# Two 256-column matmuls for each 512-column matmul of the down products in a hybrid decoder trunk

## The chip, the cores and the metric

The kernel runs on one core of one Trainium2 chip. The metric is the device time of one execution in microseconds (us), measured by the host's runs; the profile is one further execution recorded by the hardware profiler. Engines are named as in the profile: PE is the matrix engine (PEld its loading of stationary weights, which overlaps the matmuls), DVE the vector engine, ACT the scalar engine, POOL and SP the other two, SP issuing nearly all DMAs. A change of 0.2% is 3.7 us here.

## The reference

A decoder trunk of two layers over 512 tokens of width 1024. Each layer adds half a SwiGLU channel mixer, then a token mixer (latent attention in layer 0, sparse attention in layer 1), then half a second channel mixer; a norm ends it. The change touches the four channel mixers alone:

```python
def swiglu(x, w_gate, w_up, w_down):
    return (jax.nn.silu(x @ w_gate) * (x @ w_up)) @ w_down

for i in range(DEPTH):                      # DEPTH = 2
    h = h + 0.5 * swiglu(rmsnorm(h, ffn_norm_a[i]), ffn_a_w_gate[i], ffn_a_w_up[i], ffn_a_w_down[i])
    ...                                     # token mixer
    h = h + 0.5 * swiglu(rmsnorm(h, ffn_norm_b[i]), ffn_b_w_gate[i], ffn_b_w_up[i], ffn_b_w_down[i])
return rmsnorm(h, final_norm)
```

The hidden width is 2816, 22 blocks of 128. `@ w_down` is what the text calls the down product.

## The kernel before

Activations lie transposed: channels on the 128 partitions, the 512 tokens along the free axis, so the residual is eight tiles `h` of 128x512. A matmul of full precision is made as three in a rounded format: each operand is split into a high part (ACT copies it, `split`, L205) and a low part (DVE subtracts, L206), and `mm3` (L195) issues high weights by high data (L197), high by low (L198) and low by high (L199) into one PSUM bank.

A channel mixer is `ffn` (L424). For hidden blocks 0 to 2 gate and up are plain products: `plain1` (L396, matmuls L401 to L403) makes each 512-column bank in two halves of 256 columns, left and right tokens apart. For blocks 3 to 21 `wsums` (L341) and `product` (L381, matmuls L386 to L388) make the two from seven products over quarter blocks, all 256 columns wide, into the banks `px`, `pq` and `pg`. ACT copies the partial sums out (L543 to L550); a later product goes on in the same bank, so PE's product 6 into `px` waits for ACT's L543. `gate` and `act` (L430, L440) then make the activated block, split as `ah[f]` and `al[f]`, tiles of 128x512.

The down product of three finished hidden blocks and one of the eight output chunks is a `unit` (L459): SP loads a slab `wdr`, ACT and DVE split it into the two tiles `wd` (three buffers each), `down` (L451) issues three times `mm3`, nine matmuls of 512 columns, into a bank `pd`, and `add` (L456) adds that bank to the residual on DVE. Eight units belong to three hidden blocks; two or three of them follow each block's seven products on PE (L556). One such stretch of units is called a down run below. The last four hidden blocks of a mixer are multiplied at its end, chunk by chunk, with slabs from `wslab` (tile `w`). The fourth mixer ends in `last` (L582) instead: there the activations are the stationary operand and the weight slabs the moving one; the last bank of its last token block is made in two parts of 256 columns, 24 matmuls on L612 to L614.

The prediction speaks of where tiles lie in a partition. `wtiles` shifts slabs by `PAD` = 16 elements, 64 bytes, by kind:

```python
o, d = {"x": (0, 0), "act": (3 * PAD, 0), "half": (PAD, 2 * PAD)}[kind]
return t[:, o : o + 1024], t[:, o + d + 1024 : o + d + 2048]
```

"half" slabs feed the 256-column products, "act" slabs the 512-column products with `ah` and `al`. By the built program's allocation the byte address of every `ah`, `al`, `wd` and "act" tile leaves 192 on division by 256, high and low parts alike. The `x` and `four` tiles, the moving data of the 256-column products, leave 0, and their weight tiles leave 64 or 192. The text calls the address of the weights that are loaded next, less that of the data that moves meanwhile, modulo 256, the **offset**: it is 0 in the 512-column down products and 64 or 192 in every 256-column product of the mixers. In `last`, five of six loads have offset 0 and the sixth 128.

The order on each engine is set when the program is built, by a scheduler that goes by estimated durations; `issue_after` fixes some points. Each engine runs its own list in order.

Of the kernel before, what the change touches and what calls it, by code (L numbers as in the profile page):

```python
# [19 lines left out]
S = 512  # L20
# [26 lines left out]
HS = S // 2  # L47
# [14 lines left out]
class Kern:  # L62
# [361 lines left out]
    def ffn(self, idx, gain_next, ap, tp):  # L424
        nc, a = self.nc, self.a
        self.scr, self.fp = (tp, "sq", 1), tp
        ah, al, ht, row = {}, {}, [], None
# [22 lines left out]

        def down(p, w, b0, b1):  # L451
            for k in range(b0, b1):
                last = self.mm3(p, w[0][:, k - b0], w[1][:, k - b0], ah[k], al[k], k == b0, k == b1 - 1)
            return last

        def add(c, p):  # L456
# [2 lines left out]
        def unit(tag, b0, c):  # L459

            w = [ap.tile([P, NG * P], F32R, tag=t, bufs=3, name="wd").rearrange("p (k c) -> p k c", c=P) for t in ("dh", "dl")]
            raw = ap.tile([P, NG * P], F32, tag="dr", bufs=2, name="wdr")
            nc.sync.dma_start(raw, a["w_down"][idx, c, :, b0 * P : (b0 + NG) * P])
            with self.tc.issue_after(self.spread.ins) if idx % 2 and not b0 else nullcontext():
                self.split(raw.rearrange("p (k c) -> p k c", c=P), *w)
            p = self.bank(tag, "pd")
            down(p, w, b0, b0 + NG)
            add(c, p)
# [61 lines left out]
        for f in range(PLAIN, NF):  # L530
# [6 lines left out]
            w = self.wsums(idx, f)  # L537
            x, q, g = self.bank("S", "px")[:, :HS], self.bank("mm", "pq")[:, :HS], self.bank("T", "pg")
# [20 lines left out]
        if gain_next == "fin":  # L559

            hs, out = [self.parts(self.four(F32)) for _ in range(4)], []
            for t in range(4):
                for b in range(2):
                    p = self.mm_bank("ph")
# [9 lines left out]
        for c in self.order:  # L574
            p = self.mm_bank("pd")
            down(p, self.wslab(a["w_down"][idx, c, :, tail * P :], (NF - tail, P), "act"), tail, NF)
            add(c, p)
            self.norm_chunk(c)
            if ahead and c == self.order[-1]:
                self.ahead.append(ahead())  # L580
# [942 lines left out]
```

## Time and profile before

| what | value |
|---|---|
| median of three runs | 1866.52 us (1866.4 to 1866.85) |
| the profiled execution, its own time | 1865.65 us |
| span in the profile, first to last instruction | 1863.9 us |
| granted PE clock, mean | 0.999 |
| PE busy | 1849.9 us, 99% of the span, 12448 matmuls |
| PEld busy | 1686.5 us, 90% |
| DVE busy | 1506.2 us, 81% |
| ACT busy | 1068.5 us, 57% |

The four channel mixers run from about 0 to 356, 546 to 884, 884 to 1222 and 1520 to 1863 us. A matmul's duration in the profile is longer than the time until the next one starts, since matmuls overlap in the array; what a matmul costs a stream is the spacing of starts, read from the timeline. In the grouped view each row gives line, engine, operation, output<-inputs, shape and count, then busy us and mean ns of one, then the idle time ahead of the group.

### The profile page before, as it was taken

The numbers are of one execution on the slowest core, as the hardware profiler recorded it, in microseconds if no ns is written. First come the engines' busy times: TensorE is split into PE (matmuls) and PEld (weight loads), VectorE is DVE, ScalarE is ACT, GpSimd is POOL, SyncE is SP. The second block draws the span as 40 slices with busy tenths as digits, with TensorE's granted clock in tenths as the row PEclk, the third lists the DMA queues.
The fourth block names the chain that finished last, engine by engine and source line by source line (L and its number), as shares of the span: only waits on it lengthen the run. The fifth ranks groups of instructions, "written<-read, shape, count | busy, mean of one in ns | idle before, by whom it ended". The sixth has DMA issues, their size and how long they took to land.

```text
span 1863.9 us, 32992 instructions
## 1 busy us (share of the span) xinstructions
PE 1849.9 (99%) x12448; PEld 1686.5 (90%) x12448; DVE 1506.2 (81%) x2810; ACT 1068.5 (57%) x1997; POOL 297.4 (16%) x370
## 2 busy tenths in 40 slices
PE   9999999999999999999999999999999999999998
PEld 9999999878889999998999999988888889999997
DVE  8988886688779888886898887676878888888885
ACT  7555553577666555554655555445776865555554
POOL 0000000258830000001000000022666620000000
PEclk9999999999999999999999999999999999999999
DMA  6333331334433333322433332162433133333321
GB/s 238 125 114 102 102 91 47 117 103 105 115 124 112 116 102 104 112 74 64 142 120 110 107 107 80 44 180 84 108 109 103 41 118 122 114 104 105 104 78 69
DMA packets 84335, 196.38 MB, mean 105 GB/s; under 512 B 10944, under 2 KB 38464, under 8 KB 84176
## 3 DMA queue, kind: packets, MB, share of 16 engines
q1 hardware_dynamic: 81664, 191.34, 33.7%
q10 hardware_dynamic: 2512, 2.93, 0.5%
q8 instruction: 98, 1.61, 0.4%
q14 instruction: 61, 0.50, 0.1%
HBM read 178.44 MB, written 2.16 MB: 97 GB/s over the span
## 4 chain that ended last, share of the span: by engine, by line
PE 92%; DVE 3%; ACT 1%; issue 1%; POOL 1%; DMA 1%; SPq 0%; ACTq 0%; DVEq 0%; POOLq 0%
PE pd L198 8%; PE pd L197 8%; PE pd L199 8%; PE px L386 6%; PE px L388 5%; PE px L387 5%; PE pg L386 4%; PE pg L387 4%; PE pg L388 4%; PE pq L386 4%; PE pq L387 4%; PE pq L388 4%; PE o L1326 2%; PE pt L1299 2%; PE po L197 1%; PE po L199 1%
## 5 line engine op out<-in xcount | busy, mean ns | idle before, releaser
L198 PE MATMUL pd<-al,wd 128*128 128x512 f32 x576 | 225.1, 391 | 0.0
L197 PE MATMUL pd<-ah,wd 128*128 128x512 f32 x576 | 224.9, 390 | 0.0
L199 PE MATMUL pd<-ah,wd 128*128 128x512 f32 x576 | 224.6, 390 | 0.0
L289 POOL TENSOR_TENSOR s<-s,sq 128x512 f32<-128x512 f32 x38 | 54.9, 1445 | 1051.2 <-ACT sq L285 1051.2
L206 DVE TENSOR_TENSOR w<-wr,w 128x1024 fp32r<-128x1024 f32 x72 | 88.1, 1224 | 132.9 <-ACT w L205 132.6
L386 PE MATMUL px<-four,wh 128*128 128x256 f32 x608 | 168.4, 277 | 0.4 <-ACT pg L543 0.3
L388 PE MATMUL px<-four,wl 128*128 128x256 f32 x608 | 168.1, 277 | 0.2 <-DVE wl L206 0.2
L386 PE MATMUL pq<-four,wh 128*128 128x256 f32 x608 | 167.9, 276 | 0.0
L387 PE MATMUL px<-four,wh 128*128 128x256 f32 x608 | 167.9, 276 | 0.0
L388 PE MATMUL pq<-four,wl 128*128 128x256 f32 x608 | 167.8, 276 | 0.0
L387 PE MATMUL pq<-four,wh 128*128 128x256 f32 x608 | 167.8, 276 | 0.0
L457 DVE SCALAR_TENSOR_TENSOR h<-pd,h 128x512 f32<-128x512 f32 x216 | 147.5, 683 | 13.7 <-PE pd L199 13.6
L205 ACT ACTIVATE wd<-wdr 128x384 fp32r<-128x384 f32 x192 | 99.2, 519 | 98.5 <-ACT wd L205 58.2
L199 PEld LDWEIGHTS pd<-ah,wd 128*128 128x128 f32 x576 | 108.2, 188 | 22.7
L176 ACT ACTIVATE w<-wr 128x1024 fp32r<-128x1024 f32 (+3 forms) x89 | 80.8, 908 | 82.9 <-PE pd L199 19.2
L197 PEld LDWEIGHTS pd<-ah,wd 128*128 128x128 f32 x576 | 108.1, 188 | 20.5
L198 PEld LDWEIGHTS pd<-al,wd 128*128 128x128 f32 x576 | 108.1, 188 | 19.5
L178 DVE TENSOR_TENSOR w<-wr,w 128x1024 fp32r<-128x1024 f32 (+3 forms) x75 | 78.4, 1046 | 48.9 <-ACT w L176 48.7
L717 ACT ACTIVATE p<-p,small 128x512 f32<-128x512 f32 (+2 forms) x192 | 106.9, 558 | 19.1 <-DVE small L716 15.4
L386 PEld LDWEIGHTS px<-four,wh 128*128 128x128 f32 x608 | 114.1, 188 | 1.7 <-ACT pg L543 0.8
L388 PEld LDWEIGHTS px<-four,wl 128*128 128x128 f32 x608 | 114.1, 188 | 0.8 <-DVE wl L206 0.6
L386 PEld LDWEIGHTS pq<-four,wh 128*128 128x128 f32 x608 | 114.1, 188 | 0.4 <-ACT uq L545 0.4
(379 smaller groups left out, 6153.9 us busy)
## 6 DMA issues: line engine op xcount, KB each, us to landing
wr<-in_w_gu SPq DMA_DIRECT2D x93, 512.0 KB, 3.3
ru<-in_w_gu SPq DMA_DIRECT2D x76, 512.0 KB, 4.1
wdr<-in_w_down SPq DMA_DIRECT2D x192, 192.0 KB, 2.4
wr<-in_w_down SPq DMA_DIRECT2D x24, 256.0 KB, 2.6
wr<-in_mla_w_o SPq DMA_DIRECT2D x8, 512.0 KB, 3.6
th<-btab_d SPq DMA_DIRECT2D x16, 256.0 KB, 3.8
wr<-in_nsa_w_q SPq DMA_DIRECT2D x8, 512.0 KB, 3.9
wr<-in_nsa_w_o SPq DMA_DIRECT2D x8, 512.0 KB, 3.8
```

The costliest lines, as they stand in the source:

```text
L176: self.copied = nc.scalar.activation(wh[:, m], raw[:, m], AF.Copy)
L178: nc.vector.tensor_tensor(wl[:, m], raw[:, m], f32v(wh[:, m]), op=ALU.subtract)
L197: mm(out, wh, xh, start=first, stop=False)
L198: mm(out, wh, xl, start=False, stop=False)
L199: return mm(out, wl, xh, start=False, stop=last)
L205: nc.scalar.activation(hi, src, AF.Copy)
L206: (nc.gpsimd if pool else nc.vector).tensor_tensor(lo, src, f32v(hi), op=ALU.subtract)
L386: mm(out, wh[:, p], xh, start=first and p == 0, stop=False, skip_group_check=True)
L387: mm(out, wh[:, p], xl, start=False, stop=False, skip_group_check=True)
L388: mm(out, wl[:, p], xh, start=False, stop=last and p == KP - 1, skip_group_check=True)
L457: nc.vector.scalar_tensor_tensor(self.h[c], p, 0.5, self.h[c], op0=ALU.mult, op1=ALU.add)
L717: nc.scalar.activation(p_sb[:, :n], p_sb[:, :n], AF.Exp, bias=nm, scale=-1.0, accum_out=sm)
```

## The change

Inside `down`, each 512-column `mm3` becomes two triples of 256 columns, first for the left half of the bank and then for the right half. The weights and the order of the hidden blocks stay; nothing else in the kernel is edited. `down` serves the units and the mixers' ends, not `last`.

```diff
         def down(p, w, b0, b1):
             for k in range(b0, b1):
-                last = self.mm3(p, w[0][:, k - b0], w[1][:, k - b0], ah[k], al[k], k == b0, k == b1 - 1)
+                wh, wl = w[0][:, k - b0], w[1][:, k - b0]
+                for x in range(0, S, HS):
+                    o, xh, xl = p[:, x : x + HS], ah[k][:, x : x + HS], al[k][:, x : x + HS]
+                    nc.tensor.matmul(o, wh, xh, start=k == b0 and x == 0, stop=False, skip_group_check=True)
+                    nc.tensor.matmul(o, wh, xl, start=False, stop=False, skip_group_check=True)
+                    last = nc.tensor.matmul(o, wl, xh, start=False, stop=k == b1 - 1, skip_group_check=True)
             return last
```

Lines after it are five higher in the changed kernel (L543 is L548 there). The first place is PE at the start of a down run of the first mixer, behind the last product into `pg`; `pd` is the down bank, `wd` with the lower number the high weights. Before:

```order
L387 MATMUL pg_2006<-x_153,wh_1996 128x256
L388 MATMUL pg_2006<-x_153,wl_1997 128x256
L197 MATMUL pd_2109<-ah_1277,wd_2103 128x512
L198 MATMUL pd_2109<-al_1278,wd_2103 128x512
L199 MATMUL pd_2109<-ah_1277,wd_2104 128x512
L197 MATMUL pd_2109<-ah_1456,wd_2103 128x512
L198 MATMUL pd_2109<-al_1457,wd_2103 128x512
```

And PE at the same place now:

```order
L387 MATMUL pg_2204<-x_153,wh_2194 128x256
L388 MATMUL pg_2204<-x_153,wl_2195 128x256
L456 MATMUL pd_2307<-ah_1376,wd_2301 128x256
L457 MATMUL pd_2307<-al_1377,wd_2301 128x256
L458 MATMUL pd_2307<-ah_1376,wd_2302 128x256
L456 MATMUL pd_2307<-ah_1376,wd_2301 128x256
L457 MATMUL pd_2307<-al_1377,wd_2301 128x256
L458 MATMUL pd_2307<-ah_1376,wd_2302 128x256
L456 MATMUL pd_2307<-ah_1582,wd_2301 128x256
L457 MATMUL pd_2307<-al_1583,wd_2301 128x256
```

The three matmuls of a hidden block stand twice, and the loads of weights, one ahead of each matmul, are six instead of three. Otherwise PE's order is the same in the whole program, but for a few matmuls that change places in the first two blocks of the first mixer.

The scheduler also moves some instructions on the other engines, in the channel mixers alone. The second place is ACT in the second mixer, around 610 to 616 us of the profile before: `wd<-wdr` are splits of down slabs that wait for SP's loads, `pg<-px` is the copy for which PE's product 6 waits. Before:

```order
L205 ACTIVATE wd<-wdr 128x384
L205 ACTIVATE wh<-s_7358 128x512
L205 ACTIVATE wd<-wdr 128x384
L205 ACTIVATE ah<-tu 128x512
L205 ACTIVATE wd<-wdr 128x384
L543 ACTIVATE pg<-px 128x256
L205 ACTIVATE wh<-ru 128x1024
L545 ACTIVATE uq<-pq 128x256
```

And ACT there now:

```order
L205 ACTIVATE wd<-wdr 128x384
L205 ACTIVATE wh<-s_7958 128x512
L205 ACTIVATE wh<-ru 128x1024
L205 ACTIVATE wd<-wdr 128x384
L205 ACTIVATE ah<-tu 128x512
L548 ACTIVATE pg<-px 128x256
L205 ACTIVATE wd<-wdr 128x384
L550 ACTIVATE uq<-pq 128x256
```

The copy `pg<-px` now stands ahead of the third slab's split instead of behind it, and the split `wh<-ru` has moved ahead of two slab splits. On DVE the matching subtractions move by one or two places in most blocks; on SP a `wdr` load changes places with a load of gate or up weights in a few blocks at the start of each mixer; POOL keeps its order.

## The prediction

> **What bounds the kernel now.** I read the page first, for the engine that sets the time: its busy times.
>
> ```profile
> span 1863.9 us, 32992 instructions
> PE 1849.9 (99%) x12448; PEld 1686.5 (90%) x12448; DVE 1506.2 (81%) x2810; ACT 1068.5 (57%) x1997; POOL 297.4 (16%) x370
> ```
>
> PE is busy 99% of the span, so what counts is how fast matmuls follow each other. The groups by form give what the change touches.
>
> ```profile
> L198 PE MATMUL pd<-al,wd 128*128 128x512 f32 x576 | 225.1, 391 | 0.0
> L197 PE MATMUL pd<-ah,wd 128*128 128x512 f32 x576 | 224.9, 390 | 0.0
> L199 PE MATMUL pd<-ah,wd 128*128 128x512 f32 x576 | 224.6, 390 | 0.0
> ...
> L199 PE MATMUL pd<-ah,w 128*128 128x512 f32 x96 | 37.3, 389 | 0.0
> L197 PE MATMUL pd<-ah,w 128*128 128x512 f32 x96 | 37.3, 389 | 0.0
> L198 PE MATMUL pd<-al,w 128*128 128x512 f32 x96 | 37.3, 389 | 0.0
> ```
>
> 3 x 576 + 3 x 96 = 2016 wide matmuls become 4032 narrow ones, and PE idles ahead of none of them (last column). What a narrow one costs against a wide one is a matter of spacing, so next come three stretches in the view by windows, whose columns are length, then busy us with the count: one inside a down run, one inside the seven products, and the 256-column end of `last`.
>
> ```profile
> 114.44:118.52 4.08, 4.08 (x19) 1.00 0.76 210
> 120.16:128.32 8.16, 8.16 (x74) 1.00 0.22 65
> 1854.25:1856.84 2.59, 2.59 (x23) 1.00 0.40 154
> ```
>
> The counts take in matmuls begun before the stretch; by the timeline's starts there are 18, 72 and 22 spacings. Wide ones in a down run: 4.08 / 18 = 226.7 ns. Narrow ones in the products: 8.16 / 72 = 113.3 ns, exactly half. Narrow ones in `last`: 2.59 / 22 = 117.7 ns, 4.4 ns more. The clock column is 1.00 in all three. The same windows for PEld:
>
> ```profile
> 114.44:118.52 4.08, 3.38 (x18) 1.00 0.76 210
> 120.16:128.32 8.16, 8.16 (x73) 1.00 0.22 65
> ```
>
> Loading weights pauses 17% of the time in a wide run, never in a narrow one: there one load follows another. The change takes that pause away, so a load that is held up has nowhere to hide.
>
> **The narrow matmuls.** Which of the two narrow spacings will down's have? The grouped view of the two stretches shows the same split in the mean durations: 276 ns in the products, up to 282 in `last`.
>
> ```profile
> L388 PE MATMUL pq<-four,wl 128*128 128x256 f32 x8 | 2.2, 276 | 0.0
> L386 PE MATMUL px<-four,wh 128*128 128x256 f32 x8 | 2.2, 276 | 0.0
> ```
>
> ```profile
> L614 PE MATMUL pd<-w,al 128*128 128x256 f32 x4 | 1.1, 282 | 0.0
> L612 PE MATMUL pd<-wh,ah 128*128 128x256 f32 x4 | 1.1, 282 | 0.0
> L613 PE MATMUL pd<-wl,ah 128*128 128x256 f32 x4 | 1.1, 282 | 0.0
> ```
>
> What sets `last` apart from the products is the offset (weights to be loaded against data that moves, modulo 256 bytes): 0 in five of six loads there, 64 or 192 in every product. Wide matmuls run clean at offset 0. The new narrow ones take `ah`, `al`, `wd` and "act" slabs as they lie, so nearly all of their offsets are 0, as in `last`. My reading is that a load and a moving stream that start in the same place of the memory's pattern collide, that a wide matmul is long enough to absorb the delayed load, and that a narrow one is not. The timeline shows the size and that it doesn't die away.
>
> ```profile
> 1854.25 0.28 PE L612 MATMUL pd<-w,ah 128*128 128x256 f32 x1
> 1854.36 0.28 PE L613 MATMUL pd<-w,ah 128*128 128x256 f32 x1
> ...
> 1854.96 0.27 PE L612 MATMUL pd<-w,ah 128*128 128x256 f32 x1
> 1855.07 0.28 PE L613 MATMUL pd<-w,ah 128*128 128x256 f32 x1
> ...
> 1855.66 0.28 PE L612 MATMUL pd<-w,ah 128*128 128x256 f32 x1
> ...
> 1856.38 0.27 PE L612 MATMUL pd<-w,ah 128*128 128x256 f32 x1
> ```
>
> From 1854.36 to 1854.96 five take 0.60 us, 120 ns each (6.7 over 113.3); from 1854.96 to 1855.66 six take 0.70, 116.7 each (3.4 over); from 1855.66 to 1856.38 six take 0.72, 120 each. The short spacing of 0.11 at 1854.96 stands right behind the load of offset 128, of which down has almost none. So I take 5.5 ns per narrow matmul, between the mean of 4.4 and the 6.7 of the regular pieces; the ends are 3.4 and 6.7. A gain per matmul is excluded: the products' 113.3 is what a narrow stretch takes when nothing holds it up, and it is half of a wide one's.
>
> The first 86 us don't pay all of it: there DVE is busy 44.55 of 46 us, so a slower PE mostly eats waits for it.
>
> ```profile
> 40.00:86.00 46.00, 45.99 (x325) 41.67 (x325) 44.55 (x68) 26.05 (x45) 0.00 (x0) 1.00 0.34 108
> ```
>
> The six units that PE's order has there are 54 wide, 108 narrow matmuls; I count them as free (0.6 us if that cover is gone). The other 3924 cost 3924 x 5.5 = **+21.6 us** (13.3 to 26.3).
>
> The Trainium skill's page "TensorE: Matmul & The Clock Gate", section "Step-by-step: what each phase is for", says that PE reads moving data and weights through two independent ports and that loading the next weights takes no read bandwidth from the running matmul. By that rule this term is 0 and the time is that of the first rival; the 117.7 ns of `last` speak against it here.
>
> **What goes: the start of a down run.** A change of width is followed by some longer spacings.
>
> ```profile
> 112.60 0.39 PE L197 MATMUL pd<-ah,wd 128*128 128x512 f32 x1
> ...
> 114.67 0.39 PE L197 MATMUL pd<-ah,wd 128*128 128x512 f32 x1
> ...
> 116.71 0.39 PE L197 MATMUL pd<-ah,wd 128*128 128x512 f32 x1
> ```
>
> The first nine of this run take 2.07 us, the next nine 2.04: 0.03 us. The other way, from wide to narrow:
>
> ```profile
> 118.52 0.40 PE L199 MATMUL pd<-ah,wd 128*128 128x512 f32 x1
> 118.75 0.28 PE L386 MATMUL px<-x,w 128*128 128x256 f32 x1
> ...
> 120.16 0.28 PE L386 MATMUL pq<-four,wh 128*128 128x256 f32 x1
> ```
>
> Twelve products take 1.41 us against 12 x 113.3 = 1.36: 0.05 us. There are 73 down runs after the first 86 us (19 blocks in each of four mixers, less the first three). The 0.03 is part of the wide runs and goes: **-2.2 us**. The 0.05 I keep: after a run that never settled, the products have to settle again. It is -3.7 more if they need not.
>
> **What the scheduler moved.** Of the stalls, one has its cause in an order that changes: ACT sat 2.72 us before a slab split whose load was late, with the copy behind it for which PE waited.
>
> ```profile
> 615.13 0.53 ACT L205 ACTIVATE wd<-wdr 128x384 fp32r<-128x384 f32 x1 [2.72 <-DMA wdr<-in_w_down]
> 615.56 0.37 ACT L543 ACTIVATE pg<-px 128x256 f32<-128x256 f32 x1
> ```
>
> ```profile
> 615.42 0.28 PE L388 MATMUL pq<-four,wl 128*128 128x256 f32 x1
> 615.98 0.39 PE L386 MATMUL px<-four,wh 128*128 128x256 f32 x1 [0.28 <-ACT pg L543]
> ```
>
> PE's two starts lie 0.56 us apart in place of 0.11, and the restart costs about another 0.1. With the copy ahead of the split this goes: **-0.6 us**. What is late next there is `wh<-ru`, now ahead of two slab splits: it waits on DVE, not on a load. The other moves I cost at 0, within 0.6 either way, the size of this one: ACT and DVE have room (57% and 81%), and PE waits for none of them in a regular block. The low weights are now wanted 0.23 us after a unit's start in place of 0.45; their splits for the run at 128.32 lie well ahead:
>
> ```profile
> L206 DVE TENSOR_TENSOR wd<-wdr,wd x3: 546/547/558, 118.1 to 122.7; 128x384 fp32r<-128x384 f32 x3
> ```
>
> The last begins 5.6 us before that run; without this cover 0.23 us would come in each unit. The change adds no wait and no DMA, and `add` comes at a unit's end as before.
>
> **Sum.** +21.6 - 2.2 - 0.6 = +18.8 us. The profiled execution took 1865.65 us (its span 1863.9 and 1.75 around it), 0.87 less than the median of the runs, 1866.52. So 1884.5 for such an execution and **1885.3 us** as a median; ends 3.4 and 6.7 ns give 1877 and 1890.
>
> **Rivals.**
> First, on the other side: the narrow down matmuls settle at once at 113.3 ns, as 72 in a row do in the products. Then all of PE's stream in a mixer has one width, both start-ups go (73 x 0.08 = 5.8), and with the stall 6.4 us are won: **1860.1 us**. It decides below 2.8 / 3924 = 0.7 ns per matmul. For it: only 24 matmuls show offset 0, and L401 to L403 alternate halves just as the new code does. Against it: 24 in a row didn't settle, where the products need about ten.
> Second, they settle slowly, about 20 long spacings in each run: 73 x 20 x 5.5 = 8.0 - 2.8 = +5.2, **1871.7 us**.
> Third, they settle as the products do, at 0.05 us a run: 3.7 - 2.8 = +0.9, **1867.4 us**, no change that can be measured (0.2%, 3.7 us, is about what a measurement can tell from none).
> Fourth, a fixed cost of each matmul. Rows: 72 narrow in 8.16 us and 18 wide in 4.08 leave at most 0.02 / 36 = 0.6 ns for each one more, 1.2 us in all, **1867.1 us** with the stall gone. The Trainium skill's section "Back-to-back issue gap" of the same page gives columns / 2.4 + 2.5 ns; 2016 x 2.5 = 5.0 us by that estimate, 1870.9.
>
> **How the numbers follow.** Chances: forecast 0.72, first rival 0.15, second 0.07, third 0.04, fourth 0.02. The range 1870 to 1891 holds the forecast with its ends (and the 0.6 of other moves) and the second rival, about 0.79. Faster by over 0.2% is the first rival, 0.15; within 0.2% are the third and the fourth as the rows bound it, 0.06; slower are the forecast and the second, 0.79.
>
> **What would show it.** Right: the narrow `pd` groups at 280 to 282 ns, a spacing of 117 to 120 ns over a whole down run, and a first unit no slower than the later ones. Wrong: a mean of 276 and 113.3 ns in the later units (rival one or two, by where the long spacings end), a new idle time ahead of `pd` or `px` rows, or product 6 at 615 us still waiting for the copy.

## The result and the profile after

The changed kernel took 1890.88 us (median of 4 runs, 1889.80 to 1891.21) beside 1866.68 us for the kernel before on the same chip: ratio 1.0125 as estimated from all the runs, 95% interval [1.0113, 1.0138] (the two medians alone give 1.0130). It is slower by 24.2 us; the forecast of 1885.3 was 5.6 short, and the time lies inside the range by 0.1 us only. The page of the kernel after:

```profile
span 1889.3 us, 37031 instructions
PE 1874.4 (99%) x14464; PEld 1792.1 (95%) x14464; DVE 1507.4 (80%) x2810; ACT 1066.9 (56%) x1997; POOL 297.4 (16%) x370
```

DVE, ACT and POOL have what they had; PE has 2016 more matmuls and 24.5 us more busy time, and PEld's share rises from 90% to 95%. The groups by form name the place:

```profile
L457 PE MATMUL pd<-al,wd 128*128 128x256 f32 x1152 | 326.0, 283 | 0.0
...
L386 PE MATMUL pq<-four,wh 128*128 128x256 f32 x608 | 167.9, 276 | 0.2 <-ACT uq L550 0.2
...
L458 PE MATMUL pd<-ah,w 128*128 128x256 f32 x192 | 54.3, 283 | 0.0
```

All narrow `pd` rows of `down` read 283 ns, one more than the 280 to 282 that the prediction named; the products still 276. The timeline gives the spacing in a down run of the first mixer:

```profile
114.66 0.28 PE L388 MATMUL pg<-x,wl 128*128 128x256 f32 x1
114.77 0.28 PE L456 MATMUL pd<-ah,wd 128*128 128x256 f32 x1
114.89 0.28 PE L457 MATMUL pd<-al,wd 128*128 128x256 f32 x1
...
118.01 0.28 PE L456 MATMUL pd<-ah,wd 128*128 128x256 f32 x1
...
121.13 0.28 PE L458 MATMUL pd<-ah,wd 128*128 128x256 f32 x1
121.25 0.28 PE L386 MATMUL px<-x,w 128*128 128x256 f32 x1
...
122.64 0.28 PE L386 MATMUL pq<-four,wh 128*128 128x256 f32 x1
```

From 114.77 to 121.25 lie 54 matmuls: 120.0 ns each, the first 27 (to 118.01) like the last 27. Nothing settles. The windows view of two stretches of the same kernel, the run and the products behind it (columns as before), shows PE and PEld both without a gap in each:

```profile
114.77:121.25 6.48, 6.48 (x57) 6.48 (x56) 6.48 (x10) 3.27 (x5) 0.00 (x0) 1.00 0.54 157
126.57:134.73 8.16, 8.16 (x72) 8.16 (x72) 6.71 (x10) 5.14 (x7) 0.00 (x0) 1.00 0.22 60
```

The clock column is 1.00 in both, so 120.0 against 113.3 is not a lower clock.

To close the account I took every spacing of PE's starts in both traces and subtracted 113.33 ns for 256 columns and 226.67 for 512. What is left is called **excess** where it is under 12 ns, and **stall** above. Sums in us:

```text
                        before   after
excess, down products     2.47   26.60    +24.13   (4032 x 6.60 ns)
excess, seven products    4.07    3.31     -0.76
excess, all else          2.28    2.46     +0.18
stalls, all              70.21   71.91     +1.70
first to last matmul   1855.91 1881.15    +25.24
```

The narrow down products are the whole story but for 1.1 us.

### The profile page after: what moved, and what is told of

Same layout as the page of the kernel before. It is cut to its first block, busy times and chain, and to the rows that moved or that the text cites. A ratio compares the mean times of both kernels' runs of the same rounds, so it can differ in the third digit from the quotient of the medians.

```text
span 1889.3 us, 37031 instructions
## 1 busy us (share of the span) xinstructions
PE 1874.4 (99%) x14464; PEld 1792.1 (95%) x14464; DVE 1507.4 (80%) x2810; ACT 1066.9 (56%) x1997; POOL 297.4 (16%) x370
## 3 DMA queue, kind: packets, MB, share of 16 engines
q8 instruction: 114, 1.87, 0.4%
## 4 chain that ended last, share of the span: by engine, by line
PE 94%; DVE 3%; ACT 1%; issue 1%; DMA 1%; POOL 0%; SPq 0%; DVEq 0%; ACTq 0%; POOLq 0%
PE pd L458 9%; PE pd L457 9%; PE pd L456 9%; PE px L386 6%; PE px L388 5%; PE px L387 5%; PE pg L386 4%; PE pg L387 4%; PE pg L388 4%; PE pq L386 4%; PE pq L388 4%; PE pq L387 4%; PE o L1331 2%; PE pt L1304 2%; PE po L197 1%; PE po L199 1%
## 5 line engine op out<-in xcount | busy, mean ns | idle before, releaser
L457 PE MATMUL pd<-al,wd 128*128 128x256 f32 x1152 | 326.0, 283 | 0.0
L458 PE MATMUL pd<-ah,wd 128*128 128x256 f32 x1152 | 326.0, 283 | 0.0
L456 PE MATMUL pd<-ah,wd 128*128 128x256 f32 x1152 | 325.9, 283 | 0.0
L458 PEld LDWEIGHTS pd<-ah,wd 128*128 128x128 f32 x1152 | 221.1, 192 | 0.0
L457 PEld LDWEIGHTS pd<-al,wd 128*128 128x128 f32 x1152 | 220.8, 192 | 0.0
L456 PEld LDWEIGHTS pd<-ah,wd 128*128 128x128 f32 x1152 | 220.8, 192 | 0.0
L206 DVE TENSOR_TENSOR wd<-wdr,wd 128x384 fp32r<-128x384 f32 x192 | 106.3, 556 | 19.5 <-ACT wd L205 19.5
```

The lines of the kernel that those rows point to most:

```text
L206: (nc.gpsimd if pool else nc.vector).tensor_tensor(lo, src, f32v(hi), op=ALU.subtract)
L456: nc.tensor.matmul(o, wh, xh, start=k == b0 and x == 0, stop=False, skip_group_check=True)
L457: nc.tensor.matmul(o, wh, xl, start=False, stop=False, skip_group_check=True)
L458: last = nc.tensor.matmul(o, wl, xh, start=False, stop=k == b1 - 1, skip_group_check=True)
```

## The experiments

Theory A is the prediction's: a load is held up at offset 0, and a narrow matmul can't hide it. Theory B is the rival that the narrow matmuls are dear in themselves, by their number, by loading each weight tile twice, or by taking the halves of a bank in turn. Places below are byte addresses modulo 256; "data" is what moves (`ah`, `al`), "weights" the slab that is loaded meanwhile. The order of instructions on all engines is that of the changed kernel in every narrow run (that of before in the wide ones), but for two slab loads that SP issues some places later ahead of the fourth mixer in the runs that shift both data and slabs.

### First four: is it the place?

For offset 64 the slabs alone are shifted by one `PAD` (64 bytes), data left at 192. In the edit `z` counts the steps of 64 bytes by which a `wd` tile is used further on, and "down" is a kind of its own for the slabs of the mixers' ends, which ask for it in place of "act":

```diff
-            w = [ap.tile([P, NG * P], F32R, tag=t, bufs=3, name="wd").rearrange("p (k c) -> p k c", c=P) for t in ("dh", "dl")]
+            w = [ap.tile([P, NG * P + 4 * PAD], F32R, tag=t, bufs=3, name="wd")[:, z * PAD : z * PAD + NG * P].rearrange("p (k c) -> p k c", c=P)
+                 for t, z in (("dh", 1), ("dl", 1))]
...
-        o, d = {"x": (0, 0), "act": (3 * PAD, 0), "half": (PAD, 2 * PAD)}[kind]
+        o, d = {"x": (0, 0), "act": (3 * PAD, 0), "half": (PAD, 2 * PAD), "down": (0, 0)}[kind]
```

> The changed kernel with its down slabs (the wd tiles and the slabs of the mixers' ends) laid one or more steps of 64 bytes further, so that every load of weights in the narrow down runs has offset 64 to the data that moves; nothing else moves on any engine. Theory A (at offset 0 the load of the next weights is held up by the moving data, and a narrow matmul is too short to hide it): the 26.6 us by which the 4032 narrow down matmuls lie above 113.3 ns in the changed kernel go, so 1890.9 - 26.6 = about 1864 us, and 1860 if the products behind each run need not settle any more (73 x 0.05 = 3.7 us); the narrow pd groups read 276 ns. Theory B (the narrow down matmuls are dearer in themselves, by their number, by weights that are loaded twice, or by the two halves of a bank taken in turn): place changes nothing, 1891 us, and pd groups at 282 to 283 ns.

Measured: 1880.07 us, ratio to before 1.0072 [1.0059, 1.0084].

Offset 128 has `z` = 2 and "down" at `PAD`.

> As the run with offset 64, but every load in the narrow down runs has offset 128 to the data that moves. Theory A as I hold it from the kernel before (256-column matmuls at offset 64 and 192 run clean, 512-column ones at offset 128 took 7.5 ns more than 226.7 in the few places that have them): 128 is a second colliding place, and for a narrow matmul no better than 0, so 1885 to 1905 us. Theory A with only offset 0 colliding: 1860 to 1864 us. Theory B (place plays no part): 1891 us, the same as the changed kernel.

Measured: 1884.72 us, 1.0100 [1.0084, 1.0115].

The other way round, the data shifted (to 0) and the slabs left at 192:

```diff
-            ah[f] = ap.tile([P, S], F32R, tag="act", bufs=4 * NG, name="ah")
+            ah[f] = ap.tile([P, S + 4 * PAD], F32R, tag="act", bufs=4 * NG, name="ah")[:, 1 * PAD : 1 * PAD + S]
```

and `al` alike.

> The changed kernel with the tiles ah and al laid 64 bytes further in place of the slabs, so that the offset in the narrow down runs is 192 while the slabs stay where the changed kernel has them. Theory A goes by the difference of the two places alone: 113.3 ns in the down runs, 1860 to 1866 us; the end of the fourth mixer, where ah and al are the stationary side, changes its offsets too, by at most about 1 us. If it is the slabs' own place that counts: 1891 us. Theory B: 1891 us.

Measured: **1863.56 us**, 0.9984 [0.9975, 0.9993]. The groups of this kernel, called the quick kernel below:

```profile
L456 PE MATMUL pd<-ah,wd 128*128 128x256 f32 x1152 | 318.3, 276 | 0.0
L457 PE MATMUL pd<-al,wd 128*128 128x256 f32 x1152 | 318.2, 276 | 0.0
L458 PE MATMUL pd<-ah,wd 128*128 128x256 f32 x1152 | 318.2, 276 | 0.0
```

The same matmuls in the same order read 276 ns instead of 283, and the timeline shows that neither a down run nor the products behind it have a start-up any more:

```profile
114.02 0.28 PE L456 MATMUL pd<-ah,wd 128*128 128x256 f32 x1
...
120.14 0.28 PE L386 MATMUL px<-x,w 128*128 128x256 f32 x1
...
121.50 0.28 PE L386 MATMUL pq<-four,wh 128*128 128x256 f32 x1
```

54 matmuls take 6.12 us, 113.3 each, and 12 products 1.36. The windows view of that run shows that the loads (second count) have no pause here either:

```profile
114.02:120.14 6.12, 6.12 (x57) 6.12 (x55) 6.12 (x10) 3.27 (x5) 0.00 (x0) 1.00 0.50 148
```

Theory B is dead: number, halves and doubled loads are all still there. But theory A is not right either, since offset 64 kept two thirds of the cost. The fourth run was meant as a dose, high parts at offset 64, low parts at 0:

> The changed kernel with the slabs' high parts moved by 64 bytes and the low parts left: of the three loads of each half, one (the low weights) keeps offset 0, the other two have 64. Theory A: a third of the 26.6 us stays if each held-up load costs its own matmul, 1890.9 - 17.7 = about 1873 us; if one held-up load disturbs the ones behind it, up to 1882; if the two free ones make the delay good again, about 1864. Theory B: 1891 us.

Measured: 1881.28 us, 1.0080 [1.0066, 1.0093]. Offset 64 turned out dear by itself, so no third of the cost could show. But the excess of the down products is 18.2 us here and 17.8 with offset 64 throughout: one load in three at offset 0 added 0.4 us, where a price of its own (6.6 in place of 4.4 ns on 1344 loads) would have added 3.0. So the prices of loads don't simply add up.

### The next four: place of the data, or offset 192?

> The changed kernel with ah and al, the wd tiles and the slabs of the mixers' ends all laid 64 bytes further: the moving data of the down runs then leaves 0 on division by 256, and the offset is 0 as in the changed kernel. Theory A, mended after the first four runs (of the offsets only 192 is clean for a narrow matmul, since 0, 64 and 128 measured 6.6, 4.9 and 5.8 ns over 113.3 and 192 measured 0.6): 1885 to 1891 us. Theory C (the place of the moving data alone counts: it leaves 192 in all the dear runs and 0 in the products and in the run with 1863.56 us): 1862 to 1865 us and pd groups at 276 ns.

Measured: 1889.58 us, 1.0122 [1.0108, 1.0136]. The groups:

```profile
L457 PE MATMUL pd<-al,wd 128*128 128x256 f32 x1152 | 326.0, 283 | 0.0
L456 PE MATMUL pd<-ah,wd 128*128 128x256 f32 x1152 | 326.0, 283 | 0.0
L458 PE MATMUL pd<-ah,wd 128*128 128x256 f32 x1152 | 325.9, 283 | 0.0
```

They are the changed kernel's rows again, with the data at 0. Theory C, the data's place alone, falls. Offset 192 with the data at 192 (`z` = 3, "down" at `2 * PAD`):

> The changed kernel with the slabs alone laid further, so that the offset is 192 and the moving data still leaves 192 on division by 256. Theory A as mended (offset 192 is clean): 1862 to 1866 us. Theory C (the place of the moving data): still dear, 4.9 to 6.6 ns on each of 4032 narrow matmuls as at the other three places of the slabs, so 1880 to 1891 us.

Measured: 1881.76 us, 1.0083 [1.0069, 1.0096]. The mended theory A falls as well. The control with longer tiles and no shift:

> The changed kernel with the tiles ah and al made 256 bytes longer but used from their start: the distance from one to the next is as in the run with 1863.56 us, data and slabs leave 192 on division by 256 as in the changed kernel. Theories A and C: no change to the changed kernel, 1890 to 1892 us. If it was the distance between the tiles and not the 64 bytes that made that run quick: 1863 to 1865 us.

Measured: 1890.96 us, 1.0133 [1.0117, 1.0148], the changed kernel's time; the distance between tiles plays no part. Last of these, the kernel before with its data and slabs moved to 0:

> The kernel before, with its 512-column matmuls, and ah, al, wd and the end slabs 64 bytes further, so that the moving data leaves 0 and the offset is 0. It asks what the narrow matmuls bring once the data lies well. If the products behind a down run start late because the data before them lay badly: the 4.0 us that the narrow run with 1863.56 us saves there (4.7 to 0.7 us over 113.3) are saved here too, and the wide runs' own 2.5 us may go: 1860 to 1863 us, level with the narrow kernel or ahead of it. If they start late because of the change of width: 1866 us, as the kernel before, and the narrow matmuls with well-placed data are worth about 3 us.

Measured: 1864.32 us, 0.9991 [0.9982, 0.9999]. The products' excess falls from 4.07 to 2.19 us, the wide runs' own stays (2.47 to 2.15). So about half of the products' start is owed to the places of the data and slabs ahead of them, with the width as it was. The narrow kernel at 1863.56 and this one overlap in their intervals: with well-placed data, what the narrow matmuls themselves bring is not told apart from nothing.

### The last four: the pair

> The changed kernel with ah and al alone laid 192 bytes further: the moving data of the down runs leaves 128 on division by 256, the slabs stay at 192. What is left after eight runs is theory E: it is the pair of places that counts, clean where the data leaves 0 and the weights that are loaded leave 64 or 192 (the products, and the run with 1863.56 us), dear in the six other pairs, at 4.2 to 6.7 ns a matmul. If that pattern repeats every 128 bytes (0 and 128 alike, 64 and 192 alike): clean, 1862 to 1865 us. If it repeats every 256 bytes and data at 128 is as bad as data at 192: 1880 to 1891 us.

Measured: 1883.27 us, 1.0086 [1.0071, 1.0101].

> The changed kernel with ah and al 64 bytes further (data at 0) and the slabs 192 bytes further (weights at 128). Theory E with a period of 128 bytes: weights at 128 are as weights at 0, 6.6 ns a matmul, 1888 to 1891 us. With a period of 256 bytes and 0 alone bad for data at 0: 1862 to 1865 us. In between, as the single loads of weights at 128 behind the products showed (4.2 ns): about 1880 us.

Measured: 1884.40 us, 1.0092 [1.0077, 1.0107]. Neither pattern repeats every 128 bytes. All pairs that a run gave to every narrow down matmul, and the products' own, by excess per matmul (the sum over the down products divided by 4032; the products' from the steady part of their runs). The expectations name 4.9, 5.8 and 0.6 ns for three of them; by this account they are 4.4, 5.4 and 0.3:

```text
data  weights  offset   ns over 113.3   where
   0   64, 192  64, 192       0.0       the products, before
   0     192      192         0.3       data shifted by 64 (1863.56 us)
   0     128      128         5.2       1884.40 us
   0       0        0         6.6       1889.58 us
 128     192       64         4.5       1883.27 us
 192       0       64         4.4       1880.07 us
 192      64      128         5.4       1884.72 us
 192     128      192         4.4       1881.76 us
 192     192        0         6.6       the changed kernel
```

Offset 0 costs 6.6 and offset 128 costs 5.2 to 5.4, with the data at 0 and at 192 alike; offsets 64 and 192 cost 4.4 to 4.5 with the data at 128 or 192, and 0.3 or less with the data at 0. It is the pair that counts (theory E). A memory pattern in which both streams fetch would do this; the table shows the cost, not that cause. The loads' own rows speak for a held-up load only in part. PEld in the changed kernel, the quick kernel and the run with 1881.76 us, in this order:

```profile
L458 PEld LDWEIGHTS pd<-ah,wd 128*128 128x128 f32 x1152 | 221.1, 192 | 0.0
L458 PEld LDWEIGHTS pd<-ah,wd 128*128 128x128 f32 x1152 | 216.3, 188 | 0.0
L458 PEld LDWEIGHTS pd<-ah,wd 128*128 128x128 f32 x1152 | 216.2, 188 | 0.0
```

At offset 0 a load reads 4 ns longer. In the third run it reads as in the quick kernel, though each matmul costs 4.4 ns. What waits there is open.

Then one bad load in three in the units, on top of the quick kernel's edit (`z` as in `("dh", 0), ("dl", 1)`, the ends' slabs left):

> The run with 1863.56 us (data at 0, slabs at 192), with the low parts of the units' slabs alone moved to 0: one load in three of the units becomes bad, 1152 of 4032 in all. Theory E with each bad load costing its own 6.6 ns: 1863.6 + 1152 x 6.6 = 7.6, so about 1871 us, and the row that grows is the one during which the low weights are loaded, high weights by low data (L457), while L456 and L458 stay at 276 ns. If the matmul that uses the low weights is the dear one: the same sum, on L458. If the two clean ones make the delay good: 1864 us. If the disturbance spreads to all three: up to 1886 us.

Measured: 1878.64 us, 1.0061 [1.0046, 1.0076]: 15.1 us over the quick kernel, twice the 7.6 of the expectation's first case and within its last (up to 1886). The groups:

```profile
L458 PE MATMUL pd<-ah,wd 128*128 128x256 f32 x1152 | 325.6, 283 | 0.0
L457 PE MATMUL pd<-al,wd 128*128 128x256 f32 x1152 | 323.3, 281 | 0.0
L456 PE MATMUL pd<-ah,wd 128*128 128x256 f32 x1152 | 320.9, 279 | 0.0
```

All three rows grow, and the one that was to grow alone, L457, not most. Excess per matmul, counted from its own start to the next one: 2.0 ns on L456, 3.8 on L457, 7.3 on L458, whose own weights were the badly placed ones. So the cost reaches matmuls whose own pairs are clean. How it gets there isn't shown.

The good narrow pair in wide matmuls (the kernel before, data at 0):

> The kernel before, with 512-column matmuls, and ah and al 64 bytes further: data at 0 and slabs at 192, the pair that was clean for 256 columns. If a pair is good or bad whatever the width: 1862 to 1866 us. If the width has a pattern of its own, as 64 matmuls of 512 columns with data at 0 or 192 and weights at 192 elsewhere in the program showed 4.0 ns and those with data and weights both at 0 or both at 192 about 0: 2016 x 4.0 = +8.1, about 1874 us, so that what is good for one width is bad for the other.

Measured: 1868.95 us, 1.0009 [0.9999, 1.0020], not told from the kernel before. The groups still show something:

```profile
L199 PE MATMUL pd<-ah,wd 128*128 128x512 f32 x576 | 226.9, 394 | 0.0
L198 PE MATMUL pd<-al,wd 128*128 128x512 f32 x576 | 225.8, 392 | 0.0
L197 PE MATMUL pd<-ah,wd 128*128 128x512 f32 x576 | 223.6, 388 | 0.0
```

L199 went from 390 to 394 ns, L197 from 390 to 388. In sum the excess grew from 2.47 to 4.72 us: 1.1 ns a matmul, not 4.0. My expectation from 64 wide matmuls elsewhere was four times too high, but its sign holds: the pair that is clean for 256 columns is the less good one for 512, and the two pairs that cost a narrow matmul 6.6 ns (both at 0, both at 192) cost a wide one at most 0.1 ns in a steady run.

The best of all runs is the changed kernel with `ah` and `al` 64 bytes further, 1863.56 us: faster than before by 0.16% [0.07%, 0.25%], and 27.3 us under the median of the changed kernel (27.4 under the control with longer tiles). That is within the 0.2% set as the limit of a single measurement, though its interval lies below 1.

## Why the prediction was right, and where it was wrong

**5.5 ns per narrow matmul: sign right, size too small.** It measured 6.60, just below the upper end of 6.7. I took a value between two figures of `last`. Among the 24 matmuls there, two spacings inside the stretch are short (0.11 us, at 1854.96 and 1856.38), and those behind each are 3.7 to 5.7 ns over. The prediction has the first right behind the load of offset 128. The timeline of before doesn't bear that out: that load runs two matmuls ahead, while `wl` moves, the one slab of `last` that lies elsewhere.

```profile
1854.72 0.28 PE L613 MATMUL pd<-wl,ah 128*128 128x256 f32 x1
1854.84 0.28 PE L614 MATMUL pd<-wh,al 128*128 128x256 f32 x1
```

The spacing during that load is 0.12 us, and behind the next such load, at 1855.42, no short one follows. The regular pieces of 120 ns were the steady value, and down has one pair of places throughout: the mean had a part in it that down lacks. 4032 x 6.60 = 26.6 against 21.6, the largest part of the miss. That the time still lay inside the range, by 0.1 us, was luck in part: it held 0.6 us for other moves, the stalls came out 2.3 above the forecast, and 0.8 less excess in the products, which nothing had forecast, made up for some of that.

**Offset 0 as the cause: half right.** The forecast stood on it, and it named a real bad place (6.6 ns in both runs that have it). That the products run clean because their offset is 64 or 192 was wrong: the same offsets cost 4.4 ns when the data lies at 192. I had only products with data at 0 and `last` with data at 192, so two things changed together in the rows that I compared, and I named one.

**Wide absorbs, narrow doesn't: held for the pairs of the forecast, not as a rule.** Where both widths have data and weights at 0, or both at 192, a wide matmul pays at most 0.1 ns in a steady run and a narrow one 6.6. But the shift of `ah` and `al` to 0 also moves the weights of `last`, where most of the moving slabs lie at 192. Its 512-column row of before, and the same row in the quick kernel:

```profile
L614 PE MATMUL pd<-w,al 128*128 128x512 f32 x14 | 5.5, 390 | 0.0
L619 PE MATMUL pd<-w,al 128*128 128x512 f32 x14 | 5.6, 397 | 0.0
```

Its spacing goes from about 1 to about 8 ns over 226.7, and does so in every run with `ah` and `al` at 0. That is more than the 4.4 that a narrow matmul pays with data at 192 and weights at 0. So a wide matmul doesn't absorb every pair; each width has dear pairs of its own.

The Trainium skill's page "TensorE: Matmul & The Clock Gate", section "Step-by-step: what each phase is for", has loading and moving read through independent ports without cost to each other. The runs disagree on the cost: the same matmuls and loads in the same order took 113.6 ns or 119.9 ns a piece, by where two tiles lie. They don't show which part of the engine or the memory makes it.

The first rival came true only where the pair was made clean, and then in part: nothing settles behind the runs, and all excess falls by 4.4 us (from 8.82 to 4.38) where the rival had 5.8. But the stalls grow by 2.3 us where it had 0.6 less, so the time was 1863.56 and not 1860.1. The price of a narrow matmul as such, the fourth rival, is at most 0.3 ns there, below its bound of 0.6.

**The first 86 us as free: wrong.** I counted 108 matmuls as hidden behind DVE. They paid their price: excess of the down products up to 86 us went from 0.22 to 0.71 us. And the moved instructions cost there, as the first settled block shows. The start of its products in the timeline of before:

```profile
87.31 0.28 PE L386 MATMUL px<-x,w 128*128 128x256 f32 x1
```

In that of after:

```profile
89.18 0.28 PE L386 MATMUL px<-x,w 128*128 128x256 f32 x1
```

And in that of the quick kernel:

```profile
88.86 0.28 PE L386 MATMUL px<-x,w 128*128 128x256 f32 x1
```

Of the 1.87 us, 1.1 are stalls and the rest is dearer spacings. The quick kernel has no dear matmuls and is still 1.55 later than before, nearly all of it stalls. The new order of instructions, which both share, is the likely cause; it wasn't run with wide matmuls.

**-2.2 for the starts of wide runs: right,** within what can be told: their whole excess of 2.47 us is gone, as part of the +24.13. **The 0.05 us behind a run, kept: right in the main;** the products' excess fell only from 4.07 to 3.31. In the quick kernel it falls to 0.68, by 3.4 where I had said 3.7.

**-0.6 for the stall of mixer 2: right at its place.** ACT now copies for product 6 ahead of the slab split that waits for its load:

```profile
622.71 0.37 ACT L548 ACTIVATE pg<-px 128x256 f32<-128x256 f32 x1 [1.83 <-PE px L388]
623.76 0.53 ACT L205 ACTIVATE wd<-wdr 128x384 fp32r<-128x384 f32 x1 [0.68 <-DMA wdr<-in_w_down]
```

Product 6 of the same block on PE starts on time:

```profile
623.87 0.28 PE L386 MATMUL px<-four,wh 128*128 128x256 f32 x1
623.98 0.28 PE L387 MATMUL px<-four,wh 128*128 128x256 f32 x1
```

The spacing is 0.11 us in place of 0.56 and a restart. What was late next was not `wh<-ru`, as I wrote, but the same sort of split in mixer 3. ACT's timeline of after:

```profile
954.70 0.53 ACT L205 ACTIVATE wd<-wdr 128x384 fp32r<-128x384 f32 x1 [1.26 <-DMA wdr<-in_w_down]
955.13 1.04 ACT L205 ACTIVATE w<-wr 128x1024 fp32r<-128x1024 f32 x1
956.08 0.37 ACT L555 ACTIVATE pg<-px 128x256 f32<-128x256 f32 x1
```

And PE's:

```profile
955.87 0.28 PE L388 MATMUL pq<-four,wl 128*128 128x256 f32 x1
956.50 0.39 PE L386 MATMUL pg<-x,wh 128*128 128x256 f32 x1 [0.35 <-ACT pg L555]
```

The copy L555 stands behind two splits, the first of which waits 1.26 us for a load. PE loses 0.51 us there and 0.11 at the restart. In the eleven narrow traces, all with this order, that stall is between 0 and 1.02 us (six have it), and seven have one like it in the fourth mixer; the three wide ones have neither. Why the load lands later I did not follow.

**Other moves at 0, within 0.6: wrong.** All stalls together grew by 1.70 us, that is 2.3 beside the 0.6 that went; 1.1 of this lie in the first 86 us. **The sum.** Term by term against the forecast: +5.0 on the narrow matmuls (26.6 against 21.6), -0.3 on the wide starts (-2.47 against -2.2), -0.8 on the products, +2.3 on the stalls (1.70 against -0.6), +0.2 elsewhere, together +6.4, which is 25.2 against 18.8. Between the medians the miss is 5.6, since the profiled execution of before lay 0.87 us under its median and that of after (1891.09) 0.21 over.

## What to carry to other kernels

Before a matmul stream is cut into shorter pieces, look at where both of its operands lie in memory, modulo 256 bytes here, and look for rows that share that pair and the new width. A pair that is clean for one width may be dear for the other: both at 192 cost a wide matmul at most 0.1 ns and a narrow one 6.6. That the weight loads lose their pauses (17% in the wide runs) is a warning and no proof: the quick kernel's loads have none and its matmuls ran at 113.3 ns, while wide ones of `last`, with 512 columns, paid 8. If the only rows that match are few, take their regular stretches and not their mean. A shift of a tile by 64 bytes is cheap to try and moved this kernel by 27 us, so try it before a change of this sort is given up, or credited.

## What the runs showed of the hardware

For 256-column matmuls with a load of 128 columns each, the spacing depends on the pair of places modulo 256 bytes, as in the table: 113.3 ns to 119.9, lowest with the data at 0 and the weights at 64 or 192, and in no pair with the data at 128 or 192 that was run under 117.7. Data at 0 and data at 128 differ (0.3 and 4.5 ns with the weights at 192), which I had not expected. For 512 columns, in the steady part of a run, both at 0 or both at 192 cost at most 0.1 ns, data at 0 with weights at 192 about 2 (from -0.8 on L197 to 5.1 on L199), and in `last` data at 192 with weights at 0 from 5.6 to 9.3. The price of a pair doesn't add up by loads: one load in three at offset 0 cost 12.2 ns each among clean ones ((15.11 - 1.07) us of excess / 1152), nearly twice the 6.6 of a run of them, and next to nothing among loads of offset 64. Data at 64 wasn't tried in the down products, nor high and low data at different places. Why the pairs differ stays open.
